# Modulation weights of the attention stage: from SyncE's DMA queue to GpSimd's

## The chip, the cores and the metric

The kernel runs on one core of a Trainium2 chip. The core has five engines with instruction queues of their own: TensorE (PE in the rows, with its weight loads as PEld), VectorE (DVE), ScalarE (ACT), GpSimd (POOL) and SyncE (SP, which here only issues transfers). Sixteen DMA engines serve the transfers of all queues. The metric is device microseconds of one execution; the times given are the median over runs.

## The reference, cut to what matters

One block of a diffusion transformer on 256 tokens of width 2048, with 256 context tokens. All values are 32-bit floats.

```python
def adaln(cond, w, b):
    mod = jax.nn.silu(cond) @ w + b
    return [m[:, None, :] for m in jnp.split(mod, 6, axis=-1)]
...
        sh1, sc1, g1, sh2, sc2, g2 = adaln(c, w_ada[l], b_ada[l])
        mods_c = adaln(c_ctx[None, :], w_ada[l], b_ada[l])
        hc = modulate(rms_norm(ctx, norm1_g[l]), mods_c[0], mods_c[1])
...
        h = modulate(rms_norm(x, norm1_g[l]), sh1, sc1)
        u_a, v_a, q, k, v = mixer_inputs(h, w_in[l], q_norm_g[l], k_norm_g[l], True)
        a_out = chunk_gmlp(u_a, v_a, gmlp_ln_g[l], gmlp_ws[l], gmlp_bs[l])
        attn = diff_attention(q, jnp.concatenate([k_c, k], axis=1), jnp.concatenate([v_c, v], axis=1), lam)
        x_new = x + g1 * merge_mixers(a_out, attn, subln_g[l], lam_init, w_out[l])
        h2 = modulate(rms_norm(x_new, norm2_g[l]), sh2, sc2)
        x_new = x_new + g2 * peer_ffn(h2, peer_wq[l], peer_keys[l], peer_u[l], peer_v[l])
```

The six modulation vectors are products of one vector of 2048 with a matrix of 2048 x 12288: 16.8 MB of weights for each vector. The first two (shift and scale of the first norm) are needed before the projections. The next three are the subject here: g1 (m = 2), sh2 (m = 3) and sc2 (m = 4). The last, g2, is needed only at the end.

## The kernel before, in words

Large weights come in raw blocks of 128 x 1024 floats (512 KB). `load` (L113) takes one of five `raw` buffers (L42) and issues the transfer on SyncE's queue (L115). `split` (L120) makes two rounded parts of a block: ScalarE casts it to `hi` (L125), VectorE subtracts to get `lo` (L126); there are three buffers of each (L41). TensorE multiplies with both parts (L129 to L136). Both split instructions are given a high priority in the order that the scheduler writes for each engine.

The token projections (`tok_chunk`, L385) run over eight blocks of 512 columns each for k, v and q, 24 matmuls of 512 columns to a block when four token tiles are worked on. The attention stage (L608 to L621) then runs 16 units of softmax, transposes and output products, with the remaining projections as fillers between them.

The modulation vectors m = 2, 3 and 4 are computed beside this work, piece by piece. `fill` (L356) advances one of two chains by a step of one k of 16; the lists `FK`, `FV`, `N4` and `N3` say after which block or unit how many steps are traced.

- `adaln_dve` (L271) does m = 2 and m = 3: two loads of 128 x 1024 floats per step (L276), each followed by an accumulation on VectorE (L279 for the first k, L281 for the others). Its VectorE instructions are tied behind the last split by `issue_after` (L359). At the end four matmuls (L285) sum over the partitions.
- `adaln_pe` (L288) does m = 4: two loads per step (L293), each followed by matmuls with 32 stationary columns (L296).

Both take their target from the same two buffers with the tag `ra` (L275, L292), so that a load can start only when the instruction that reads the buffer's earlier content is done. Both pick the issuing queue by the constant `RQ` (L48):

```python
r = work.tile([P, 1024], F32, tag="ra", name="ra", bufs=2)
{'g': G, 's': S, 'y': nc.sync}[RQ].dma_start(r, wada[m - 2, k, i])
```

With `'y'` these 64 + 32 loads stand in SyncE's queue, between the raw blocks of the projections and of the attention stage. Each queue works in its order: an instruction that waits holds those behind it.

GpSimd's queue in this part of the program holds eight products of the rotary embedding (L415 in `qk_post`, L393), each of which VectorE's L416 waits for, and through it the transposes at L421. Later it holds the loads of the sixth modulation vector (L257 in `adaln_g2`), and later still the gathers of the expert rows (L941).

Of the kernel before, what the change touches and what calls it, by code (L numbers as in the profile page):

```python
# [44 lines left out]
UJ = [0, 2, 4, 5, 7, 8, 9, 11, 12, 13, 14, 15]  # L45
UE = 5
DL = 1
RQ = 'y'  # L48
ANCH = 1
LEAD = 3  # L50
RL = 6
# [17 lines left out]
def dit_block(ctx: ExitStack, tc: tile.TileContext, xT, ctxT, cT, wad1, wada, bada, n1g, n2g,  # L69
# [201 lines left out]
    def adaln_dve(m):  # L271
        acc = work.tile([P, D], F32, tag="ada", name="ada", bufs=1)
        for k in range(KT):
            for i in range(2):
                r = work.tile([P, 1024], F32, tag="ra", name="ra", bufs=2)  # L275
                {'g': G, 's': S, 'y': nc.sync}[RQ].dma_start(r, wada[m - 2, k, i])  # L276
                a = acc[:, i * 1024:(i + 1) * 1024]
# [10 lines left out]
    def adaln_pe(m):  # L288
        acc = n512()
        for k in range(KT):  # L290
            for i in range(2):
                r = work.tile([P, 1024], F32, tag="ra", name="ra", bufs=2)  # L292
                {'g': G, 's': S, 'y': nc.sync}[RQ].dma_start(r, wada[m - 2, k, i])  # L293
                for jj in range(2):
# [947 lines left out]
```

## Time and profile before

| | us |
|---|---|
| median of 3 runs | 2056.96 |
| lowest and highest run | 2055.96, 2059.11 |
| time of the profiled execution | 2050.24 |
| its span, from the first to the last instruction | 2048.3 |
| TensorE busy | 1965.5 (96% of the span) |
| VectorE busy | 1638.8 (80%) |
| ScalarE busy | 1009.4 (49%) |
| GpSimd busy | 414.9 (20%) |

The rows that stand below come from the profiled execution alone, whose time differs from the median by 6.7 us. A busy TensorE is not TensorE at its peak, since matmuls are pipelined and their ends are modelled. Instructions that only issue a transfer are not counted as busy. Releasers of a wait are inferred from semaphore events; where several were needed, the one that came last is named.

### The profile page before, as it was taken

Reading aid. Unit: us, or ns where it says so; the run is one execution under the profiler, and the core shown is the slowest. Engines: PE = TensorE matmul, PEld = TensorE weight load, DVE = VectorE, ACT = ScalarE, POOL = GpSimd, SP = SyncE. Lnnn points to the kernel's source line nnn. Section 1 sums busy time; section 2 is a strip of 40 time slices with the busy share of each in tenths; the row PEclk is TensorE's granted clock in tenths of the full one; section 3 lists DMA queues with packets and bytes.
Section 4 is the critical chain, followed back from the end, with each engine's and each line's share of the span. In section 5 each row is a group of like instructions: output and inputs, shape, how many; then the busy total and the mean of one; then the engine's idle time right before and its main releaser. Section 6 shows DMA issues by size and latency. Waiting matters only on the chain.

```text
span 2048.3 us, 29826 instructions
## 1 busy us (share of the span) xinstructions
PE 1965.5 (96%) x11182; PEld 1626.8 (79%) x11182; DVE 1638.8 (80%) x2344; ACT 1009.4 (49%) x1393; POOL 414.9 (20%) x315
## 2 busy tenths in 40 slices
PE   4999999999999999899999999999999999999998
PEld 0457775566998777899988988888898888888876
DVE  5338667776667777777788999999999999999897
ACT  3224314555546333389655545544554455445452
POOL 0001000000000232299322222221222223222200
PEclk9999999999999999999999999999999999999999
DMA  8786688676567776567999999999999999999994
GB/s 329 264 317 231 209 270 274 228 256 210 199 186 250 234 272 225 186 211 263 319 369 376 380 376 355 384 381 376 373 379 374 367 367 368 393 356 367 391 326 158
DMA packets 173744, 622.03 MB, mean 304 GB/s; under 512 B 17824, under 2 KB 44704, under 8 KB 154528
## 3 DMA queue, kind: packets, MB, share of 16 engines
q1 hardware_dynamic: 119232, 434.16, 59.4%
q0 software_dynamic: 23040, 151.01, 19.0%
q10 hardware_dynamic: 31328, 34.97, 5.1%
q8 instruction: 87, 1.43, 0.3%
q14 instruction: 57, 0.47, 0.1%
HBM read 603.30 MB, written 16.78 MB: 303 GB/s over the span
## 4 chain that ended last, share of the span: by engine, by line
PE 75%; DVE 11%; DMA 9%; issue 2%; ACT 2%; POOL 1%; ACTq 0%; DVEq 0%; POOLq 0%
PE z L131 10%; PE z L130 10%; PE z L132 10%; PE n L135 9%; PE m L135 7%; PE z L1079 5%; PE z L1080 5%; DVE lo L126 4%; DMA ra<-in_wada 4%; PE n L136 4%; PE m L136 3%; PE z L1025 2%; DMA raw<-in_vt 2%; DMA raw<-in_ut 2%; PE n L237 2%
## 5 line engine op out<-in xcount | busy, mean ns | idle before, releaser
L125 ACT CAST hi<-raw 128x1024 fp32r<-128x1024 f32 x656 | 688.6, 1050 | 859.7 <-PE z L1079 163.3
L126 DVE TENSOR_TENSOR lo<-raw,hi 128x1024 fp32r<-128x1024 f32 x656 | 798.9, 1230 | 223.1 <-ACT hi L125 201.5
L135 PE MATMUL n<-big,hi 128*128 128x384 f32 x1120 | 333.9, 362 | 0.1
L136 PE MATMUL n<-big,lo 128*128 128x192 f32 x1120 | 284.8, 254 | 12.2 <-DVE lo L126 12.0
L135 PE MATMUL m<-big,hi 128*128 128x384 f32 x928 | 273.6, 359 | 0.0
L130 PE MATMUL z<-hi,big 128*128 128x512 f32 x608 | 246.6, 406 | 2.7 <-DVE vtok L468 1.7
L131 PE MATMUL z<-lo,big 128*128 128x512 f32 x608 | 242.4, 399 | 1.3 <-DVE lo L126 1.0
L132 PE MATMUL z<-hi,big 128*128 128x512 f32 x608 | 238.5, 395 | 0.0
L136 PE MATMUL m<-big,lo 128*128 128x192 f32 x928 | 234.2, 252 | 1.4 <-DVE lo L126 1.4
L136 PEld LDWEIGHTS n<-big,lo 128*128 128x128 f32 x1120 | 215.7, 193 | 19.4 <-DVE lo L126 16.1
L135 PEld LDWEIGHTS n<-big,hi 128*128 128x128 f32 x1120 | 212.4, 190 | 3.8 <-ACT hi L125 0.3
L941 POOL DMA_INDIRECT big<-in_vtab,iu x64 | 130.9, 2045 | 363.9 <-DVE big L957 336.3
L941 POOL DMA_INDIRECT big<-in_utab,iu x64 | 107.2, 1674 | 390.8 <-DVE big L949 377.1
L136 PEld LDWEIGHTS m<-big,lo 128*128 128x128 f32 x928 | 177.0, 191 | 6.8 <-DVE lo L126 3.5
L135 PEld LDWEIGHTS m<-big,hi 128*128 128x128 f32 x928 | 174.6, 188 | 3.5
L130 PEld LDWEIGHTS z<-hi,big 128*128 128x128 f32 x608 | 114.2, 188 | 48.6 <-issue 21.0
L957 DVE SCALAR_TENSOR_TENSOR big<-big,gate 128x2048 f32<-128x2048 f32 x63 | 147.8, 2345 | 0.0
L132 PE MATMUL z<-big,lo 128*128 128x256 f32 (+1 forms) x512 | 144.5, 283 | 2.4 <-DVE lo L126 2.4
L949 DVE SCALAR_TENSOR_TENSOR big<-big 128x2048 f32<-128x2048 f32 x64 | 146.2, 2284 | 0.0
L130 PE MATMUL z<-big,hi 128*128 128x256 f32 (+1 forms) x512 | 145.7, 286 | 0.0
L131 PE MATMUL z<-big,hi 128*128 128x256 f32 (+1 forms) x512 | 144.3, 282 | 0.1
L132 PEld LDWEIGHTS z<-hi,big 128*128 128x128 f32 x608 | 114.1, 188 | 33.9 <-issue 8.7
(280 smaller groups left out, 3273.2 us busy)
## 6 DMA issues: line engine op xcount, KB each, us to landing
raw<-in_ut SPq DMA_DIRECT2D x256, 512.0 KB
raw<-in_vt SPq DMA_DIRECT2D x256, 512.0 KB
ra<-in_wada SPq DMA_DIRECT2D x96, 512.0 KB
raw<-in_wkvq SPq DMA_DIRECT2D x64, 512.0 KB
raw<-in_wad SPq DMA_DIRECT2D x42, 512.0 KB
raw<-in_wout SPq DMA_DIRECT2D x32, 512.0 KB
raw<-in_wq SPq DMA_DIRECT2D x32, 512.0 KB
big<-in_wada POOLq DMA_DIRECT2D x32, 512.0 KB, 4.0
```

The source lines that it names most:

```text
L125: hi_at[0] = S.copy(hi, raw)
L126: anchor[0] = V.tensor_sub(lo, raw, hi)
L130: mm(ps, ah, bh, start=first, stop=False)
L131: mm(ps, ah, bl, start=False, stop=False)
L132: mm(ps, al, bh, start=False, stop=last)
L135: mm(ps[:, :2 * n], wh, act[:, :, :n], start=first, stop=last)
L136: mm(ps[:, :n], wl, act[:, 0, :n], start=False, stop=last, skip_group_check=True)
L941: G.indirect_dma_start(out=gbufs[n % 3], out_offset=None, in_=(utab if n < GT else vtab), in_offset=bass.IndirectOffsetOnAxis(ap=iu[:, s:s ...
L949: V.scalar_tensor_tensor(buf, buf, 1.0, hrow, op0=ALU.mult, op1=ALU.mult, accum_out=dots[:, s:s + 1])
L957: V.scalar_tensor_tensor(hrow, buf, gate[:, s:s + 1], hrow, op0=ALU.mult, op1=ALU.add)
L1079: mm(pb, g, hi[:, sl], start=(i == 0), stop=False)
L1080: mm(pb, g, lo[:, sl], start=False, stop=(i == NG - 1))
```

## The change

The constant that names the queue of the modulation loads of `adaln_dve` and `adaln_pe` goes from SyncE to GpSimd. The loads themselves, their two buffers and the instructions that read them stay as they are in the program's text.

```diff
--- before.py
+++ after.py
@@ -45,7 +45,7 @@
 UJ = [0, 2, 4, 5, 7, 8, 9, 11, 12, 13, 14, 15]
 UE = 5
 DL = 1
-RQ = 'y'
+RQ = 'g'
 ANCH = 1
 LEAD = 3
 RL = 6
```

## Rows read from the trace of the kernel before

**Rows 1.** Busy time by stretch, with granted clock (PEclk), DMA share and GB/s.
```profile
150.00:330.00 180.00, 171.22 (x768) 131.45 (x766) 127.64 (x152) 60.17 (x85) 11.83 (x6) 1.00 0.73 242
330.00:520.00 190.00, 181.19 (x857) 113.71 (x858) 131.50 (x244) 105.75 (x189) 3.46 (x2) 0.98 0.71 237
...
474.00:480.00 6.00, 6.00 (x15) 2.60 (x12) 3.14 (x5) 0.65 (x2) 0.00 (x0) 0.50 0.39 132
```

**Rows 2.** Waits, 150 to 530 us: who for whom, total us, times, longest.
```profile
PE n L296 <- DMA ra<-in_wada: 8.3, 7, 2.3
PE m L421 <- DVE w L417: 5.1, 5, 1.2
...
DVE ada L281 <- DMA ra<-in_wada: 33.8, 29, 5.0
...
ACT hi L125 <- DMA raw<-in_wkvq: 6.6, 1, 6.6
```

**Rows 3.** Timeline of SyncE's queue: start, us, instruction, count of merged ones.
```profile
238.77 1.52 SPq L276 DMA_DIRECT2D ra<-in_wada  x2
...
244.36 2.08 SPq L276 DMA_DIRECT2D ra<-in_wada  x2
247.25 0.33 SPq L115 DMA_DIRECT2D raw<-in_wkvq  x1
...
254.60 2.44 SPq L276 DMA_DIRECT2D ra<-in_wada  x2
...
342.96 0.38 SPq L115 DMA_DIRECT2D raw<-in_wkvq  x1
...
465.42 0.33 SPq L115 DMA_DIRECT2D raw<-in_wu  x1
466.67 0.33 SPq L293 DMA_DIRECT2D ra<-in_wada  x1
```

**Rows 4.** Timeline of VectorE; in brackets the idle time before and its releaser.
```profile
243.05 1.28 DVE L281 SCALAR_TENSOR_TENSOR ada<-ra,c,ada 128x1024 f32<-128x1024 f32 x1 [1.89 <-DMA ra<-in_wada]
244.80 1.28 DVE L281 SCALAR_TENSOR_TENSOR ada<-ra,c,ada 128x1024 f32<-128x1024 f32 x1 [0.47 <-DMA ra<-in_wada]
246.00 1.22 DVE L126 TENSOR_TENSOR lo<-raw,hi 128x1024 fp32r<-128x1024 f32 x1
...
258.95 1.29 DVE L281 SCALAR_TENSOR_TENSOR ada<-ra,c,ada 128x1024 f32<-128x1024 f32 x1 [1.13 <-DMA ra<-in_wada]
261.06 1.28 DVE L281 SCALAR_TENSOR_TENSOR ada<-ra,c,ada 128x1024 f32<-128x1024 f32 x1 [0.83 <-DMA ra<-in_wada]
...
339.69 1.22 DVE L126 TENSOR_TENSOR lo<-raw,hi 128x1024 fp32r<-128x1024 f32 x1
```

**Rows 5.** The page's DMA issues: the loads of L257, median us to landing last.
```profile
big<-in_wada POOLq DMA_DIRECT2D x32, 512.0 KB, 4.0
```

**Rows 6.** Timeline of GpSimd at the first loads of L257.
```profile
638.23 0.53 POOL L257 DMA_DIRECT2D big<-in_wada  x1 [23.94 <-PE z L265]
639.58 0.53 POOL L257 DMA_DIRECT2D big<-in_wada  x1 [0.82 <-PE z L265]
646.89 0.53 POOL L257 DMA_DIRECT2D big<-in_wada  x1 [6.78 <-DMA big<-in_wada]
```

**Rows 7.** Timeline of TensorE at a load of L293 and at one of L257.
```profile
473.64 1.92 PE L296 MATMUL n<-ra,cs 128*32 128x512 f32 x4 [2.33 <-DMA ra<-in_wada]
...
642.72 1.04 PE L265 MATMUL z<-big,cs 128*32 128x512 f32 x2
```

**Rows 8.** Instructions of line L281, 238 to 331 us: ns min/median/max, first and last start.
```profile
L281 DVE SCALAR_TENSOR_TENSOR ada<-ra,c,ada x29: 1272/1285/1286, 237.5 to 328.3; 128x1024 f32<-128x1024 f32 x29
```

**Rows 9.** Timeline of ScalarE: casts of two raw blocks one after the other.
```profile
244.38 1.05 ACT L125 CAST hi<-raw 128x1024 fp32r<-128x1024 f32 x1 [4.48 <-PE z L132]
249.92 1.05 ACT L125 CAST hi<-raw 128x1024 fp32r<-128x1024 f32 x1 [4.48 <-PE z L132]
```

**Rows 10.** Instructions of line L415: four of eight products for k, ns min/median/max.
```profile
L415 POOL TENSOR_TENSOR w<-w,tbk x4: 1699/1732/2152, 174.8 to 232.9; 128x512 f32<-128x512 f32 x4
```

## The prediction

> **What bounds the kernel now.** I read the span first, then the busy time by stretches, then the waits, and last single instructions. The change touches 96 loads of modulation weights (64 at L276, 32 at L293), which run from 153.8 to 514 us; nothing else of the program uses the constant. In the two stretches that hold them TensorE is busy for 171.22 of 180 us and 181.19 of 190 us at a mean clock of 1.00 and 0.98 [rows 1]. So TensorE sets the pace there, and all that a better path for these loads can give back directly is the idle rest, 8.8 + 8.8 = 17.6 us. The list of waits says what that rest is: 8.3 us in 7 waits of L296 for a modulation load, 5.1 us in 5 waits of the rotary transposes at L421 [rows 2]. VectorE waits four times as much for the same loads, 33.8 us in 29 waits [rows 2], but that is idle time of an engine which is not the bound.
>
> **What the change removes: nothing that waits in SyncE's queue.** The natural hope is that the loads no longer stand in one line with the raw blocks. Each load can start only when one of the two `ra` buffers is free, so I subtract the end of the instruction that frees it from the issue. The first load of the row at 244.36 follows a VectorE instruction that began at 243.05 and took 1.28, so ended at 244.33: 0.03 us late [rows 3, 4]. I did this subtraction for all 94 loads after the first two; the worst is 0.64 us. The modulation loads are therefore bound by their buffers, not by the queue. The raw blocks behind them: the one issued at 247.25 follows the split that ended at 246.00 + 1.22 = 247.22, again 0.03 [rows 3, 4]. Seven of 70 raw loads are held for 0.6 to 2.8 us; the second largest is issued at 342.96 where its buffer came free at 339.69 + 1.22 = 340.91 [rows 3, 4]. They don't matter, because in these 380 us ScalarE's cast waited for a raw block once [rows 2]. I cost the freeing of SyncE's queue at nothing; its cover is the five raw buffers, and were that cover gone the sum of the held time, 10.7 us, would be the prize.
>
> **What it adds: the time from issue to landing.** Every modulation load that someone waits for becomes later by the difference between the two paths. SyncE's path: eight loads from 238.77 to 256.71, from issue (the second of a merged row starts at its end less 0.33) to the waiting VectorE instruction, take 4.28 and 4.83 us for the first two, 4.35 and 4.35 for the last two, 4.18 in the mean [rows 3, 4]. GpSimd's path is seen only in the later load of the last modulation part, same tile shape, beside similar traffic: the page gives a median of 4.0 [rows 5]; the load at 638.23 reaches its waiting matmul at 642.72, so 4.49 [rows 6, 7]; the next one, at 639.58, holds GpSimd's own wait for it until 646.89, so 7.31, and the pair has a mean of 5.9 [rows 6]. The three readings give a difference of 4.0 - 4.18 = -0.2, 4.49 - 4.18 = +0.3 and 5.9 - 4.18 = +1.7 us. I take their mean, +0.6, since the loads of this change also come in pairs with a raw block close by, and keep -0.2 and +1.7 for the range.
>
> The Trainium skill ("DMA: Bandwidth & Descriptors", section "Specifications") gives about 1 us to the first byte on GpSimd's path and 0.6 on SyncE's. By that difference, 0.4, the sum below would be 0.2 x 7 = 1.4 us smaller.
>
> **Where that falls on the path.**
> - TensorE's own waits at L296: 7 x 0.6 = 4.2 us [rows 2], with no cover, since they are TensorE's idle time already. Ends: 7 x -0.2 = -1.4 and 7 x 1.7 = 11.9.
> - VectorE between 238 and 331 us: 29 accumulations of some 1.28 us [rows 8]. Two buffers give one pair per landing plus one accumulation: 4.18 + 1.28 = 5.46 us. TensorE uses up one raw block in 249.92 - 244.38 = 5.54 us, read from the casts, which start when TensorE frees the split buffer [rows 9]. So the pair just fits now. With +0.6 it takes 6.06, and the split that stands behind it in VectorE's order slips by 0.52 per block, 14.5 x 0.52 = 7.5 us in all. The cover is the three split buffers: the cast starts two blocks ahead of use, 11.1 us, and cast and split take 1.05 + 1.22 of it [rows 4, 9], which leaves 8.8. So 0, barely. At +1.7 the pair takes 7.16: 14.5 x 1.62 = 23.5, less 8.8, 14.7 us on the path.
> - GpSimd's queue: the loads are put beside eight rotary products of 1.7 us at L415 [rows 10]. A load that becomes ready behind one waits for up to 1.7 us; a product that becomes ready behind a load waits for its issue, 0.53 us [rows 6]. VectorE's L416 and then L421 wait for the product. Five waits of L421 could each grow by 0.53; I take one, 0.5 us. The other user of this queue, the load at L257, is at work from some 640 us on [rows 6], long after the last of the 96 at 514, so it is not held.
> - TensorE's clock: one load issued at 466.67 came late [rows 3], TensorE stood for 2.33 us until 473.64 [rows 7], and its granted clock was then 0.50 (1.2 GHz instead of 2.4) for the 6 us shown, all of them busy [rows 1]. So such a gap costs some 3 us more. Longer gaps may bring a second one, another order may lose this one. I count 0 and +-3 for the range.
> Sum: 0 + 4.2 + 0 + 0.5 = 4.7 us. The profiled execution has a time of 2050.24; the sum concerns its stretch from 153 to 520 us, after which TensorE carries any loss to the end. The median of the runs is 2056.96, 6.7 above it, and I add the sum to that: 2061.7 us.
>
> **The rivals.**
> - *No change (within 0.2%, which is 4.1 us and about what can be told from no change here).* The landing differs by 0.3 us or less: 7 x 0.3 = 2.1, so 2059. For it: the page's 4.0, and a queue that was not late. Against it: the load at 639.58 [rows 6]. The Trainium skill ("DMA: Bandwidth & Descriptors", section "Issuing engines are not separate DMA queues") says that transfers issued from several engines run on the same DMA engines and that only the sequencer's issue time is saved, which would make this rival the outcome; the trace agrees so far as the 0.33 us of an issue on SyncE is not missed by anyone.
> - *Faster.* On a path of its own a modulation load need not let a raw block issued just ahead of it through first, so the late landing at 466.67, which had a raw block issued 1.25 us ahead [rows 3], comes in 4.2 us: the 2.33 us gap shrinks to nothing and the 3 us of half clock go too. With -0.2 on the other six waits: -2.3 - 3 - 1.2 = -6.5, 2050.5. It decides if loads on GpSimd's path land in less than 4.2 us beside a raw block. Against it: 7.31 for a load in that company.
> - *Much slower.* VectorE's pair falls behind TensorE before the cover of 8.8 us can be refilled, and the splits become TensorE's wait: +11.9 + 14.7 = +26.6, 2083.6. It decides from a difference of 0.7 us on, only 0.1 above mine.
> - *It doesn't do what it says.* The order of GpSimd's queue could set a load behind a rotary product that itself is late. In the trace those products wait for VectorE or ScalarE, in the order in which VectorE also frees the buffers, so each such hold is one product, 1.7 us, at most eight times; part of the slower side.
>
> **How the numbers follow.** Slower by over 0.2%: 0.46, of which the forecast (small loss) has 0.33 and the large loss 0.13. Within 0.2%: 0.38, since 4.7 us is hardly past the bound and half the difference in landing would bring it inside. Faster by over 0.2%: 0.16, from the clock and the one late load. Cases of both signs hold much, but the likeliest has its own range of 2058 to 2067. The range of all: low 2050, the faster rival; high 2079, since the large loss needs the upper end at every load and I leave its last part out.
>
> **What would show it.** Right: the list of waits still has L296 on the load, 12 us or so; the time from a GpSimd issue to the waiting accumulation is near 4.8; SyncE's waits hold only raw blocks; TensorE's busy time by stretch is unchanged and its idle time grows in the second stretch. In the first stretch VectorE's splits start later after their casts with each block, without a wait of TensorE at L131. Wrong: landings at or under 4.2 us, or TensorE waiting for splits before 330 us; or a new order of VectorE's instructions, which no row here can show.

## The result, and the profile after the change

The changed kernel takes 2075.97 us (median of 16 runs, 2061.93 to 2083.89) against 2056.02 for the kernel before on the same chip (16 runs, 2047.66 to 2063.40): a ratio of 1.0098, 95% interval [1.0079, 1.0117], some 20 us slower. The profiled execution takes 2069.56 us with a span of 2067.8. The forecast was +4.7 us: right in sign, four times too small.

Busy time by stretch of the changed kernel (stretch, its length, PE, PEld, DVE, ACT, POOL, clock, DMA share, GB/s):

```profile
150.00:330.00 180.00, 163.71 (x723) 127.64 (x720) 121.30 (x142) 53.80 (x77) 33.56 (x49) 0.97 0.68 225
330.00:520.00 190.00, 176.84 (x817) 111.49 (x817) 130.92 (x234) 101.83 (x177) 29.82 (x52) 0.97 0.69 233
```

Against [rows 1] TensorE has 7.5 us more idle time in the first stretch and 4.4 us more in the second, and the clock is down by 0.03 and 0.01. DMA moves less per second, but not because its packets got slower. By the profile's list of DMA queues, what the change adds to the GpSimd queue (36864 - 23040 packets, 26.2% of the time of 16 DMA engines in a span of 2067.8 us, less 19.0% in 2048.3) is 0.177 us a packet, and what it takes from SyncE's queue comes to 0.176.

The DMA queues in the profile of the kernel before (packets, MB, share of the 16 engines; q0 is GpSimd's queue, q1 SyncE's):

```profile
q1 hardware_dynamic: 119232, 434.16, 59.4%
q0 software_dynamic: 23040, 151.01, 19.0%
```

and of the changed kernel:

```profile
q1 hardware_dynamic: 105408, 383.83, 51.5%
q0 software_dynamic: 36864, 201.34, 26.2%
```

The waits of the changed kernel, 150 to 530 us (who for whom, total us, times, longest):

```profile
DVE ada L281 <- DMA ra<-in_wada: 40.3, 27, 5.3
...
PE n L296 <- DMA ra<-in_wada: 10.4, 10, 2.1
...
PE z L130 <- DVE vtok L468: 8.3, 2, 4.7
PE m L421 <- DVE w L417: 8.1, 6, 3.3
...
ACT hi L125 <- DMA raw<-in_wkvq: 2.0, 1, 2.0
```

and one line of the kernel before, same stretch:

```profile
PE z L130 <- DVE vtok L468: 1.7, 2, 1.2
```

L296 waits 2.1 us more for its loads than in [rows 2], L421 3.0 us more, and a line that the prediction did not name has grown most: TensorE waits 6.6 us more for L468, VectorE's copies of finished V tiles out of PSUM (the memory that TensorE writes to) at the two chunk boundaries of the V projection. The first of them, seen on GpSimd, VectorE and TensorE of the changed kernel:

```profile
253.94 0.53 POOL L276 DMA_DIRECT2D ra<-in_wada  x1 [3.33 <-DVE ada L281]
258.14 0.53 POOL L276 DMA_DIRECT2D ra<-in_wada  x1 [3.68 <-DVE ada L281]
```

```profile
252.36 1.28 DVE L281 SCALAR_TENSOR_TENSOR ada<-ra,c,ada 128x1024 f32<-128x1024 f32 x1 [1.44 <-DMA ra<-in_wada]
...
262.12 1.28 DVE L281 SCALAR_TENSOR_TENSOR ada<-ra,c,ada 128x1024 f32<-128x1024 f32 x1 [1.94 <-DMA ra<-in_wada]
...
273.18 1.28 DVE L281 SCALAR_TENSOR_TENSOR ada<-ra,c,ada 128x1024 f32<-128x1024 f32 x1 [1.47 <-DMA ra<-in_wada]
274.38 1.28 DVE L468 COPY vtok<-z 128x512 f32<-128x512 f32 x2
```

```profile
275.12 0.80 PE L130 MATMUL z<-hi,big 128*128 128x512 f32 x1 [4.68 <-DVE vtok L468]
```

The copies stand behind an accumulation that waits for its load, and TensorE stands for the copies, since all four PSUM tiles of that kind are in use. In the kernel before it stood there for 1.23 us (below). How late the loads are: VectorE frees the buffer at 252.36 + 1.28 = 253.64, and GpSimd's issue starts at 253.94, 0.30 us later, where SyncE took 0.03. The next load, issued at 258.14, has VectorE waiting until 262.12, 3.98 us. From issue to landing the two paths do not differ on average: 4.57 us over the 96 loads against 4.52, by the landing events of the two traces (the times at which a load's last semaphore step is recorded). Long landings are not what makes this boundary late in this trace: in the 50 us ahead of it none took over 6.4 us, and of the 96 only two took over 7, issued at 153.80 and 378.63.

Comparing the starts of ScalarE's casts one by one, the changed kernel is 2.6 us late at 206 us, 8.3 after the first chunk boundary, 11.1 after the second, up to 21.5 in the attention stage, 15.3 at 580. The remaining 4 us come after 650 us, where nothing of the change is left. Most of the traces below, with the loads on SyncE too, fall back by 2 to 4 us at the same place, and the kernel before varies by 16 us from run to run, so I read nothing from that part.

One more thing changed. The scheduler orders the instructions by its own idea of when a load is ready, and with the loads on GpSimd it wrote another order for TensorE, ScalarE and VectorE. In the first rotary step VectorE now has two accumulations in the middle of the rotary chain:

```profile
174.72 1.29 DVE L281 SCALAR_TENSOR_TENSOR ada<-ra,c,ada 128x1024 f32<-128x1024 f32 x1 [1.93 <-DMA ra<-in_wada]
175.92 0.68 DVE L405 TENSOR_TENSOR w<-w,s 128x512 f32<-128x512 f32 x1
177.47 1.77 DVE L281 SCALAR_TENSOR_TENSOR ada<-ra,c,ada 128x1024 f32<-128x1024 f32 x1 [0.86 <-DMA ra<-in_wada]
179.16 0.68 DVE L414 TENSOR_TENSOR w<-w,tbk 128x512 f32<-128x512 f32 x1
```

The transposes of this step then wait 3.3 us, where they waited about 1. So there were two theories to separate first: the order (theory 1), and the loads' path (theory 2). A third was that the loads and the rotary products hold one another up on GpSimd.

### The profile page after: what moved, and what is told of

Same layout as the page of the kernel before. It is cut to its first block, busy times and chain, and to the rows that moved or that the text cites. A ratio compares the mean times of both kernels' runs of the same rounds, so it can differ in the third digit from the quotient of the medians.

```text
span 2067.8 us, 29901 instructions
## 1 busy us (share of the span) xinstructions
PE 1969.7 (95%) x11182; PEld 1631.7 (79%) x11182; DVE 1641.4 (79%) x2344; ACT 1009.8 (49%) x1393; POOL 460.6 (22%) x411
## 3 DMA queue, kind: packets, MB, share of 16 engines
q0 software_dynamic: 36864, 201.34, 26.2%
## 4 chain that ended last, share of the span: by engine, by line
PE 70%; DMA 13%; DVE 9%; issue 5%; ACT 1%; POOL 1%; ACTq 0%; DVEq 0%; POOLq 0%; SPq 0%
PE z L131 9%; PE z L130 9%; PE z L132 9%; PE n L135 9%; PE m L135 7%; DMA ra<-in_wada 6%; PE z L1079 5%; PE z L1080 5%; PE n L136 4%; DVE lo L126 4%; PE m L136 3%; PE z L1025 2%; DMA raw<-in_ut 2%; PE n L237 2%; DMA raw<-in_vt 2%
## 5 line engine op out<-in xcount | busy, mean ns | idle before, releaser
L125 ACT CAST hi<-raw 128x1024 fp32r<-128x1024 f32 x656 | 688.7, 1050 | 866.7 <-PE z L1079 170.5
L126 DVE TENSOR_TENSOR lo<-raw,hi 128x1024 fp32r<-128x1024 f32 x656 | 800.7, 1234 | 239.0 <-ACT hi L125 221.9
L130 PE MATMUL z<-hi,big 128*128 128x512 f32 x608 | 248.4, 410 | 9.9 <-DVE vtok L468 8.3
L131 PE MATMUL z<-lo,big 128*128 128x512 f32 x608 | 245.3, 404 | 3.3 <-DVE lo L126 3.0
L130 PEld LDWEIGHTS z<-hi,big 128*128 128x128 f32 x608 | 116.1, 191 | 53.1 <-issue 17.2
L131 PEld LDWEIGHTS z<-lo,big 128*128 128x128 f32 x608 | 116.4, 192 | 39.5 <-issue 11.4
L130 PE MATMUL z<-big,hi 128*128 128x256 f32 (+1 forms) x512 | 146.3, 287 | 0.0
L131 PE MATMUL z<-big,hi 128*128 128x256 f32 (+1 forms) x512 | 144.9, 283 | 0.1
```

What stands on the lines that cost most here:

```text
L125: hi_at[0] = S.copy(hi, raw)
L126: anchor[0] = V.tensor_sub(lo, raw, hi)
L130: mm(ps, ah, bh, start=first, stop=False)
L131: mm(ps, ah, bl, start=False, stop=False)
```

## The experiments

All ratios are against the kernel before on the same chip; "+x us" is the ratio times its median (2052 to 2054 us).

**Order and path apart.** Both runs force an order on TensorE, ScalarE and VectorE with edges between neighbours that carry no semaphore; `ORDER` holds one list of instructions per engine, taken from the other kernel (cut):

```diff
+    for part in zlib.decompress(base64.b85decode(ORDER)).decode().split(";"):
...
+        for a, b in zip(seq, seq[1:]):
+            tc.add_manual_dep(b, a.name, nosync, reason="order")
```

Loads on GpSimd, order of the kernel before:

> The loads go through GpSimd's queue as in the changed kernel, and TensorE, ScalarE and VectorE take their instructions in exactly the order of the kernel before (extra ordering edges without a semaphore). Theory 1 (most of the loss is the new order that the scheduler wrote for those three engines): what is left is the 0.27 us by which GpSimd issues later than SyncE after a buffer's release, times the handful of loads that TensorE waits for and times VectorE's run without slack at the two chunk boundaries of the V projection: 3 to 5 us over the kernel before, 2059 to 2061 us. Theory 2 (the loads' own path, the later issue and what VectorE then lags, costs it): the time of the changed kernel, near +20 us over the kernel before, about 2076 us.

Loads on SyncE, order of the changed kernel:

> The loads stay on SyncE's queue, and TensorE, ScalarE and VectorE take their instructions in the order of the changed kernel. Theory 1 (the order): +13 to +17 us over the kernel before, 2069 to 2073 us. Theory 2 (the loads' path): no difference that can be measured, within 3 us of the kernel before.

Measured: 1.0073 [1.0045, 1.0100], +15 us, for the path alone, and 1.0030 [1.0009, 1.0051], +6 us, for the order alone. The two add up to the whole, 21 of 20 (each is known to some 4 to 6 us). So both theories hold in part, and the larger part is the path, which I had put at 3 to 5 us. With the same order on three engines the traces of the first run and of the kernel before can be laid side by side: from 157 to 270 us their casts differ by 0.4 us at most. Then the first boundary; the kernel before (VectorE, TensorE):

```profile
267.13 1.28 DVE L281 SCALAR_TENSOR_TENSOR ada<-ra,c,ada 128x1024 f32<-128x1024 f32 x1 [0.43 <-DMA ra<-in_wada]
268.33 1.28 DVE L468 COPY vtok<-z 128x512 f32<-128x512 f32 x2
```

```profile
269.07 0.50 PE L130 MATMUL z<-hi,big 128*128 128x512 f32 x1 [1.23 <-DVE vtok L468]
```

and the loads on GpSimd in the same order (GpSimd, SyncE, VectorE, TensorE, and the stretch after TensorE's wait):

```profile
266.63 0.53 POOL L276 DMA_DIRECT2D ra<-in_wada  x1 [1.16 <-DVE ada L281]
```

```profile
267.50 0.33 SPq L115 DMA_DIRECT2D raw<-in_wkvq  x1
```

```profile
268.93 1.28 DVE L281 SCALAR_TENSOR_TENSOR ada<-ra,c,ada 128x1024 f32<-128x1024 f32 x1 [1.45 <-DMA ra<-in_wada]
273.76 1.28 DVE L281 SCALAR_TENSOR_TENSOR ada<-ra,c,ada 128x1024 f32<-128x1024 f32 x1 [3.55 <-DMA ra<-in_wada]
274.96 1.28 DVE L468 COPY vtok<-z 128x512 f32<-128x512 f32 x2
```

```profile
275.70 0.80 PE L130 MATMUL z<-hi,big 128*128 128x512 f32 x1 [7.49 <-DVE vtok L468]
```

```profile
275.70:279.10 3.40, 3.40 (x8) 2.75 (x9) 2.89 (x4) 0.00 (x0) 0.40 (x2) 0.50 0.67 171
```

The accumulation in front of the copies starts at 273.76 in place of 267.13, TensorE waits 7.49 us in place of 1.23, and after that idle time its granted clock is 0.50 (1.2 GHz) for 3.4 us, in which it does the work of 1.7. That is 6.3 + 1.7 = 8.0 us, and the next cast is 8.0 us later than before. By 580 us the run is 9.2 us late in all, so this one place holds most of what is seen ahead of the late stages. In the changed kernel, with its new order, the casts fall back by 5.7 us at this boundary, and with that order on SyncE's queue by 3.3.

The load issued at 266.63 took 7.04 us to land. A raw block was issued 0.87 us behind it on the other queue, and by the landing events the two ended together, at 273.67 and 273.87. The loads of 7.58 us at 240.61, 7.38 at 423.72 and 7.40 at 482.17 show the same: a raw block 0.7 to 0.95 us behind, both ending within 0.2 us of one another. Such a neighbour is not enough, though. In the four kernels with two buffers and the modulation loads on GpSimd, 69 loads have a raw block issued 0.7 to 0.95 us behind them; 45 of these landed in under 5 us, 8 took over 7, and the median of the 69 is 4.1. What tells the 8 from the 45 was not found. In one queue no load caught up with an earlier one: all 165 loads of SyncE's queue between 150 and 520 us in the kernel before landed in the order of their issue.

The Trainium skill ("DMA: Bandwidth & Descriptors", section "Issuing engines are not separate DMA queues") says that transfers from different engines run on the same 16 DMA engines and interleave; the pairs that end within 0.2 us of one another agree. It also says that only issue time is saved by spreading them; here spreading them cost 15 us with the order held, so it was not free.

With the raw blocks on SyncE and two buffers, landings above 7 us number 1 of 384 with the modulation loads on SyncE too (four kernels) and 17 of 384 with them on GpSimd (four kernels). Four of the 17 are the first load of all, at some 154 us, which has three raw blocks issued in the 2 us ahead of it.

**GpSimd's own work.** The rotary product L415 is moved to VectorE, once with the loads on GpSimd, once on SyncE:

```diff
-            G.tensor_tensor(p2, zn, b, op=ALU.mult)
+            V.tensor_tensor(p2, zn, b, op=ALU.mult)
```

> The changed kernel with the one product of the rotary step that GpSimd computes (L415) put on VectorE, so that nothing but loads stands in GpSimd's instruction stream there. Theory 3 (the loads' issues and that product hold one another up in GpSimd's stream): 2 to 5 us of the 20 come back, 2071 to 2074 us. Theories 1 and 2: nothing comes back, and VectorE's added 1.2 us per product in six steps costs 0 to 7 us: 2076 to 2083 us. The scheduler writes its order anew, so that only a gain speaks for theory 3.

> The kernel before, loads on SyncE's queue, with the same product put on VectorE: the comparison for the run with the loads on GpSimd's queue and that product on VectorE. Theory 3: this is 0 to 7 us slower than the kernel before and within 3 us of its companion, since without the product in GpSimd's stream the two queues are alike. Theory 1: its distance to the companion is again set by the orders that the scheduler writes, and may be anything from -5 to +20 us. Theory 2: the companion is about 20 us slower than this.

Measured: 1.0089 [1.0056, 1.0122], +18 us, with the loads on GpSimd; 0.9969 [0.9952, 0.9986], -6 us, on SyncE. The first, some 2 us under the changed kernel, is by itself no evidence against theory 3, which expected a gain of 2 to 5. But with no product left in GpSimd's stream the two queues are 25 us apart (in orders that the scheduler wrote anew), where it expected them within 3, so theory 3 falls as the account of the loss. That the kernel before gets faster was not expected: TensorE's wait for L417 drops from 5.1 us [rows 2] to 0.4.

**Late issue or two queues.** The order stays that of the kernel before in both; only the queue of the raw blocks changes, from the first rotary step to the end of the attention stage (cut; `G` is GpSimd):

```diff
     def load(src):
         r = rawp.tile([P, 1024], F32, tag="raw", name="raw")
-        nc.sync.dma_start(r, src)
+        rawq[0].dma_start(r, src)
         return r
 
+    rawq = [nc.sync]
...
+    rawq[0] = G
     kTt = big([P, H, 512])
...
     def q_first(j, half):
+        rawq[0] = nc.sync
```

Raw blocks on GpSimd, modulation loads on SyncE:

> The queues are swapped from the start of the first rotary step to the end of the attention stage: the modulation loads stay on SyncE's queue, the raw weight blocks go through GpSimd's; TensorE, ScalarE and VectorE keep the order of the kernel before, instruction for instruction. Theory A (two queues: a raw block issued about 0.9 us after a modulation load shares the DMA engines with it, and both land late, instead of one after the other): the long landings of over 7 us show up again, though the modulation loads are issued 0.03 us after their buffer's release, and 8 to 13 us are lost, most of it at the first chunk boundary of the V projection: 2061 to 2066 us. Theory B (GpSimd's 0.3 us from release to issue, in a loop of two buffers that has no slack): no long landing, a loss of 0 to 3 us, 2053 to 2056 us. Against both: GpSimd's rotary products stand behind waiting raw loads, worth up to 5 us around 180 us and 210 to 235 us, which the casts there would show.

Both on GpSimd:

> Both kinds of loads go through GpSimd's queue in that stretch, in one stream again, with the order of the kernel before on TensorE, ScalarE and VectorE. Theory A (two queues): no landing of a modulation load over 7 us between 180 and 520 us, and what is lost at the first chunk boundary of the V projection (8.0 us with the loads alone on GpSimd) falls to under 4 us: 2056 to 2060 us, apart from what the rotary products lose behind waiting loads. Theory B (the 0.3 us from release to issue): the loss stays, 10 us or more, most of it at that boundary: 2063 us or more.

Measured: 1.0044 [1.0025, 1.0063], +9 us, with the queues swapped, and 1.0041 [1.0023, 1.0059], +8 us, with both on GpSimd. TensorE at the first boundary, swapped and then both (lines were added above: L131 is the L130 of before, L470 the L468):

```profile
270.17 0.80 PE L131 MATMUL z<-hi,big 128*128 128x512 f32 x1 [2.26 <-DVE vtok L470]
```

```profile
272.70 0.79 PE L131 MATMUL z<-hi,big 128*128 128x512 f32 x1 [4.87 <-DVE vtok L470]
```

Neither theory gets its numbers. The time of the swapped run lies in theory A's range, but its landings and its boundary don't. Landings above 7 us, 5 of 96 with the loads alone on GpSimd, are down to 1 in each. What the boundary costs in all, TensorE's wait and the half clock behind it, is read from the next cast of ScalarE: the kernel before, the loads alone on GpSimd, both on GpSimd, swapped (L126 is the L125 of before):

```profile
273.54 1.05 ACT L125 CAST hi<-raw 128x1024 fp32r<-128x1024 f32 x1 [5.98 <-PE z L132]
```

```profile
281.89 1.05 ACT L125 CAST hi<-raw 128x1024 fp32r<-128x1024 f32 x1 [13.95 <-PE z L132]
```

```profile
279.65 1.06 ACT L126 CAST hi<-raw 128x1024 fp32r<-128x1024 f32 x1 [12.09 <-PE z L133]
```

```profile
276.20 1.05 ACT L126 CAST hi<-raw 128x1024 fp32r<-128x1024 f32 x1 [8.56 <-PE z L133]
```

The casts ahead of the boundary start within 0.4 us of one another, so the three runs lose 8.0, 6.1 and 2.6 us here against the kernel before. With both on GpSimd, TensorE's wait is 4.87 - 1.23 = 3.6 us longer, and it then works for 5.4 us at half clock, which is another 2.7:

```profile
272.70:278.10 5.40, 5.40 (x13) 4.23 (x14) 4.16 (x4) 0.00 (x0) 1.46 (x4) 0.50 0.67 193
```

No modulation load from 246 to 272 us of that run took over 5.0 us to land. So one queue with GpSimd's late issue loses 6.1 of the 8.0 us without any long landing, and two queues with a prompt issue of the modulation loads lose 2.6. These shares are of one execution each and are rough: at 580 us the trace with both on GpSimd is 14 us late and the one with the loads alone 9.2, though its whole time is the lower, +8 against +15. In the whole time the intervals do not separate the swapped run from the one with both on GpSimd. Why the swapped run loses 9 us is open: it is only 2.6 us late at 580 us.

**A late issue on SyncE.** A direct test of the late issue, in the order of the kernel before; the same edit is made at both loads:

```diff
-                {'g': G, 's': S, 'y': nc.sync}[RQ].dma_start(r, wada[m - 2, k, i])
+                for q in (slice(0, 16), slice(16, 128)):
+                    nc.sync.dma_start(r[q], wada[m - 2, k, i][q])
```

> All loads stay on SyncE's queue and TensorE, ScalarE and VectorE keep the order of the kernel before. Only each modulation load is issued as two, 16 rows and then 112 rows, so that its main part goes out one SyncE issue (about 0.4 us) later, as late as GpSimd would issue it (0.30 us against 0.03 us after the buffer's release), but in one queue with the raw blocks. Theory B (the late issue in a loop of two buffers without slack costs it): 5 us or more are lost at the first chunk boundary of the V projection, and the time is 6 to 15 us over the kernel before, 2058 to 2067 us. Theory A (two queues side by side, with long landings, cost it): no landing over 7 us, under 3 us lost at that boundary, 2051 to 2056 us.

Measured: 1.0195 [1.0170, 1.0220], +40 us. As a test it failed, because the scheduler rewrote SyncE's order. SyncE's timeline (L277 is the L276 of before), and ScalarE's wait for raw blocks from 150 to 530 us:

```profile
238.60 34.25 SPq L277 DMA_DIRECT2D ra<-in_wada  x24
272.89 2.44 SPq L115 DMA_DIRECT2D raw<-in_wkvq  x5
```

```profile
ACT hi L125 <- DMA raw<-in_wkvq: 72.2, 9, 13.1
```

Twelve loads in 24 pieces stand ahead of five raw blocks, which wait 34 us behind them; that run costs more than any other here, and it shows what sharing a queue can cost when the order in it is wrong. The kernel before had the raw blocks alternate with the loads [rows 3]. What a late issue alone costs in SyncE's queue is left untested.

**Taking the copies out of the way.** At both boundaries, VectorE's copies and the split behind them go ahead of the two accumulations. The two lists below stand for VectorE's instructions by their lines and are not code; all else is as in the forced order:

```diff
-L281 L281 L468 L468 L126      # first boundary; the second: L281 L468 L281 L468 L126
+L468 L468 L126 L281 L281
```

> The loads on GpSimd's queue and the order of the kernel before, with one thing moved: on VectorE, at the two chunk boundaries of the V projection, the PSUM copies L468 and the split behind them stand ahead of the two accumulations L281 that stood ahead of them. If the late loads cost time because those copies stand behind accumulations that wait for a load (TensorE's wait for them was 7.5 us at the first boundary, 1.2 us in the kernel before), that wait falls to about 1 us and 8 to 10 of the 15 us over the kernel before come back: 2058 to 2062 us. If the loss is put elsewhere (TensorE's own loads L296, the attention stage), at most 3 us come back: 2065 us or more.

> The kernel before, loads on SyncE's queue, with the same copies and splits moved ahead at the two chunk boundaries. TensorE's waits there are 1.2 us and 0.5 us, so there is little to win: 0 to 3 us below the kernel before, 2050 to 2053 us; if the two accumulations that now stand later put VectorE behind in the next blocks, up to 4 us above it.

Measured: 1.0052 [1.0029, 1.0075], +11 us, with the loads on GpSimd, and 1.0000 [0.9982, 1.0018] on SyncE. TensorE's wait for the copies is gone (0.17 us at 267.45), but of the 15 us only some 4 come back, nearer to the 3 us of a loss put elsewhere than to the 8 to 10 expected of the copies. The rest is met 57 us later on VectorE, ScalarE and TensorE of the GpSimd run:

```profile
324.59 1.28 DVE L281 SCALAR_TENSOR_TENSOR ada<-ra,c,ada 128x1024 f32<-128x1024 f32 x1 [4.25 <-DMA ra<-in_wada]
325.79 0.68 DVE L494 TENSOR_REDUCE s<-z 128x1 f32<-128x512 f32 x1
```

```profile
327.76 0.69 ACT L499 ACTIVATE w<-z,s 128x512 f32<-128x512 f32 x1 [5.00 <-DVE s L496]
```

```profile
328.59 1.59 PE L491 MATMUL z<-big 64*128 64x512 f32 x2 [4.72 <-ACT w L499]
```

VectorE is as late as it was; now the first softmax reduction stands behind the waiting accumulation, and TensorE waits 4.72 us for that. The SyncE run has the same wait at the same place (5.14 us), so what moving the copies wins it gives back. This run also bounds what the forcing itself costs: with the order of the kernel before forced but for these two places, the time is that of the kernel before, to 0.2%.

**More room in the loop.** Three buffers for the modulation loads, six w2 buffers to make space (cut; the same edit stands at each tile with the tag `ra`):

```diff
-    W2 = 7
+    W2 = 6
-                r = work.tile([P, 1024], F32, tag="ra", name="ra", bufs=2)
+                r = work.tile([P, 1024], F32, tag="ra", name="ra", bufs=3)
```

> The kernel before, loads on SyncE's queue, with three buffers for the modulation loads in place of two and six w2 buffers in place of seven (for the space). Both theories: VectorE's accumulations L281 no longer wait for their loads one buffer turn at a time, its waits for ra fall from 33.8 us to under 15 us, and the time is 0 to 8 us below the kernel before: 2045 to 2053 us. The w2 buffer that it gives up could cost a few us in the rotary steps. It is the base for the next run.

> The same three buffers with the modulation loads on GpSimd's queue, TensorE, ScalarE and VectorE in exactly the order of the run with three buffers on SyncE's queue. If the loss comes from a loop of two buffers without slack, whether by long landings (theory A) or late issues (theory B), a third buffer covers most of it: 0 to 4 us over that run, against 13.5 us with two buffers. If it comes from something that a buffer can't cover (packets of the GpSimd queue slowing the raw blocks, GpSimd's stream holding the rotary products), 8 us or more over that run.

Measured: 0.9952 [0.9935, 0.9968], -10 us, on SyncE; 0.9978 [0.9957, 0.9999], -4.5 us, on GpSimd in the same order. By these the queue costs some 5 us (the intervals allow 0 to 11) in place of 15: a third buffer covers about two thirds, somewhat less than expected. The 10 us on SyncE are those of the third buffer, the w2 buffer given up and the order that the scheduler wrote for them, which were not tried apart; VectorE's waits for `ra` fell from 33.8 to 18.0 us there, not to under 15. TensorE's wait at the first boundary is still 2.16 us on SyncE and 5.80 us on GpSimd, and one load ahead of it took 7.9 us to land, so the long landings are not covered. With three buffers they come in one queue too: 3 of 96 above 7 us on SyncE, 7 of 96 on GpSimd.

**Faster than both.** Loads on SyncE, three buffers, and L415 on VectorE:

> A version that is meant to beat both kernels: the loads on SyncE's queue, three buffers for them (six w2 buffers in place of seven), and the rotary product of GpSimd on VectorE. The first alone gave 9.9 us over the kernel before, the second alone 6.4 us. If the two act at different places (VectorE's waits for loads in the V projection and the attention stage; the rotary chain around 180 us and 210 to 235 us): 12 to 16 us below the kernel before, 2037 to 2041 us. If both win the same slack: 8 to 10 us, 2043 to 2045 us.

Measured: 2032.32 us (6 runs, 2027.87 to 2034.68), 0.9888 [0.9866, 0.9911], -23 us, more than the sum of the two alone, some 16. Its busy time by stretch, and what TensorE waits for from 150 to 530 us:

```profile
150.00:330.00 180.00, 174.36 (x787) 131.99 (x779) 131.99 (x164) 61.16 (x87) 0.00 (x0) 0.99 0.75 258
330.00:520.00 190.00, 187.04 (x1043) 134.42 (x1039) 144.99 (x262) 119.45 (x210) 0.00 (x0) 1.00 0.71 238
```

```profile
PE z L130 <- DVE vtok L468: 3.3, 2, 1.9
...
PE m L421 <- DVE w L417: 0.2, 1, 0.2
PE n L296 <- DMA ra<-in_wada: 0.2, 1, 0.2
```

The 8.3 us at L296 and the 5.1 us at L421 of [rows 2] are gone. TensorE's idle time is 5.6 + 3.0 = 8.6 us of the 17.6 that the kernel before had [rows 1]; that more came back than the 9 us between them fits the order, which the scheduler wrote anew here too, and was not tried apart.

## Why the prediction was right in sign and wrong in size

- **SyncE's queue, 0.** Held. TensorE and VectorE gained nothing from it; ScalarE's wait for raw blocks fell from 6.6 us to 2.0 (with the old order it is 8.3), in time that nobody missed.
- **Issue to landing, +0.6 us.** Too large as a mean, too kind as a spread. From issue to landing the difference is 4.57 - 4.52 = 0.05 us (0.17 with the old order). What I had not priced is the time before the issue, 0.30 us on GpSimd against 0.03: together +0.3 per load. And the mean hides the landings above 7 us, one of which I had read ([rows 6], 7.31) and averaged away. The Trainium skill ("DMA: Bandwidth & Descriptors", section "Specifications") gives about 1 us to the first byte on GpSimd's path and 0.6 on SyncE's. The measured 0.3 is near that difference, but all of it lies ahead of the issue.
- **TensorE's waits at L296, 4.2 us.** Mis-sized by half: +2.1 in the changed kernel, +2.5 with the old order.
- **VectorE in the V projection, 0. This is the step that failed**: "The cover is the three split buffers ... which leaves 8.8. So 0, barely." The slip itself was there: with the order unchanged VectorE's accumulation was 6.6 us late at the first boundary (273.76 against 267.13). That this is near my 7.5 us is luck: I had +0.6 per load turn by turn, the mean was +0.3, and 3.1 of the 6.6 came in one step, with the load of 7.04 us. What was wrong is the cover. No split with two blocks in hand stood behind it there, and TensorE waited for no split before 330 us. It was a PSUM copy whose reader was already waiting, with a cover of nothing, and when that was moved away, a softmax reduction with as little. I had priced the cover of the most frequent instruction in VectorE's order, not of the least covered one. Measured, with the loads on GpSimd in the old order: 8.0 us at the first boundary and 2.5 at the second, half-clock time included.
- **GpSimd's queue, 0.5 us.** L421's wait grew by 3.0 us, but not by the queue: with the old order it is 5.1 us as before, with the new order on SyncE's queue 7.5.
- **Clock, 0.** It cost several us in the changed kernel: from the two stretches' means, 180 x 0.03 + 190 x 0.01 = 7.3 us of full-speed time, an estimate. Summed over the half-clock stretches between 150 and 530 us, the work that TensorE lost in them is 10.8 us against 3.4 before, and each of the six stretches lies beside an idle time of 1.6 to 4.7 us. With the loads on GpSimd in the old order it is 3.3 us: the boundary brings a new stretch, but the one of [rows 1] at 474 us is gone, so there the clock cost nothing on balance, which is what the prediction had counted.
- **The order.** The prediction ended with "a new order of VectorE's instructions, which no row here can show" as what would make it wrong; it did, by about 6 us of the 20.
- **The rivals.** The large loss was the nearest one: VectorE's pair falls behind until TensorE waits. It happened with half the difference that I had named as the point from which it decides (0.7 us), and TensorE waited for the copies, not for the splits that the rival named. "No change" and "Faster" fell with the interval.

What stays open: how the 15 us of the path divide between late issues and long landings (at the first boundary only roughly known, elsewhere not at all), what makes a load land late, and what the swapped queues lose after 300 us.

## What to carry to other kernels

Where an engine runs a loop of few buffers with no slack, every delay of a load makes it late for everything in its order, whether a small one at each turn (0.3 us here) or a large one now and then. What that costs is set by the instruction with the least cover that stands behind it in that engine's order; look for that one, not for the usual one. A load that others wait for is at risk on a queue beside a stream of large loads: most landed as fast as in one queue, but long landings were 17 of 384 in place of 1. A further buffer took the cost of the second queue from 15 us to about 5, and with the order written for it gained 10 us in one queue. And a DMA's queue is an input of the scheduler: part of what such a change does is another order, which can be measured by forcing the old one.

## What was not expected of the hardware

- A DMA on GpSimd starts 0.30 us after the buffer's release, on SyncE 0.03 us; from issue to landing the means are 4.6 to 4.7 and 4.5 to 4.6 us (four kernels each, two buffers).
- Two 512 KB loads issued 0.7 to 0.95 us apart on two queues mostly don't hold up the first (45 of 69 landed in under 5 us), but some end within 0.2 us of one another, the first after 7.0 to 7.6 us. With two buffers, landings above 7 us were 17 of 384 with the two kinds of loads on two queues, and 1 of 384 in one.
